# A two-layer streaming encoder on one core: the second attention's matmuls on halves of TensorE's rows

## The chip, the core and the metric

The kernel runs on one core of one Trainium2 chip. The metric is device microseconds of one execution. Within the core, TensorE (PE) multiplies, its weight loads (PEld) run beside its matmuls; VectorE (DVE), ScalarE (ACT) and GpSimd (POOL) work on tiles of 128 rows (partitions); SyncE (SP) issues most DMAs. Each engine works off its own list of instructions in order and waits on semaphores of the others. TensorE writes PSUM, which has eight banks of 128 x 512 fp32 values.

## The reference, cut to what matters

Layer A is a banded softmax attention, layer B a "stick-breaking" attention; both with gates, projections, residuals, and a prompt of 2048 frames beside a sample of 64 new frames with 2048 cached ones. The change touches layer B's attention and the two projections that run beside it. There are 16 heads of 64 numbers.

```python
def sb_block(q, k, v, q_pos, k_pos):
    z = jnp.einsum('bqhd,bkhd->bhqk', q, k).astype(jnp.float32) * SCALE
    mask = (k_pos[None, :] < q_pos[:, None])[None, None]
    log_fail = jnp.where(mask, jax.nn.log_sigmoid(-z), 0.0)
    later = jnp.flip(jnp.cumsum(jnp.flip(log_fail, -1), axis=-1), -1) - log_fail
    w = jnp.where(mask, jnp.exp(jax.nn.log_sigmoid(z) + later), 0.0)
    return jnp.einsum('bhqk,bkhd->bqhd', w.astype(v.dtype), v)
```

The kernel never forms `w`. With f = sigmoid(-z), the running product s of f from the newest key backwards holds the chance that no later key was taken, and `w` is a difference of neighbouring s. So the output is a sum of s against differences of neighbouring rows of v (made earlier and stored as `v_b`), plus the last row of v (`ends`).

## The kernel before

fp32 values are cut into a high and a low part, both fp32r, and a product is three products of parts. Layer B runs after its projections, from about 2040 us of the span on. The prompt's 2048 queries are four groups g of 512, its keys four chunks c of 512; groups come in two parts, (1, 0) and (3, 2), and in each part the loop is over eight pairs of heads (`hp`), then groups, then the two heads h, then chunks from c = g down to 0. After a part's groups comes a sample item of that pair, whose 64 queries of both heads fill one tile.

One `item(hp, g, h, ..., c)` has four tiles t of 128 queries. For each tile:

- `scores` makes z (128 x 512) with two matmuls over all 128 rows of the array. Rows 0 to 63 hold the high parts of the keys and rows 64 to 127 the low parts; the second matmul has the query's parts exchanged, so the four products of parts come out of two passes.
- `pass_sticks` (L1339) takes f = sigmoid(-z) on ACT, and, off the diagonal, three steps one beat apart: `pairs` on POOL multiplies neighbours (`two`, 256 values), `scan` on DVE runs the product over `two` backwards into every second value of s, `between` on POOL copies the carry and fills the other values (`s<-f,s`). On the diagonal (c = g) there is one scan over up to 512 values instead, and POOL does nothing. `own`, a constant that the scan also reads, lies in a PSUM bank.
- `weigh` turns four 128 x 128 blocks of s into a PSUM bank `wt` (the turnings, L90 `wt<-ident,s`), `split` copies it out as `ph` on ACT and the rest as `pl` on DVE, and `products` adds v times each into `acc`, one bank per head. `gate_steps` closes a head's `acc` into `ot`; POOL adds `ends` and multiplies by the gate.

Around this stand the "beside" products: the late k, q and g projections (`late_job`, `ps_j`) and the output projection (`out_tile`, `ps_o`), which a `Beat` object mixes in at a rate of `RATE["b"]` steps for each tile. `Beat.beat` writes the instructions of one beat: steps of older tiles, turnings, scores of the new tile, products, beside steps. `LAG`, `HOLD` and `LEAD` set how many beats lie between them. A scheduler then sets each engine's final order from what stands in the code, so the order shown below is that of the built program. PSUM holds three `wt` banks (beside products use them too), `own`, two z and two `acc`. All calls go through the recorder of L90, so most rows of the profile have that line.

## Time and profile before

| | us |
|---|---|
| runs shown | 3278.98 and 3283.02, median 3281.0 |
| span of the profiled execution | 3278.2 |
| profiled execution's own time | not listed apart; its span is 2.8 below the median of the runs |
| layer B's attention, from its first scores to its last products | 2040 to 3185, 1145 |
| what follows it: last output products, norm, stores | 3185 to 3279, 94 |
| TensorE busy over the span | 3204.2 (98%) |
| mean granted TensorE clock | 0.994 |

A row of the grouped view reads: line, engine, operation, out<-in by the program's names, shape, count, then busy microseconds and the mean nanoseconds of one, then the engine's idle time just before and what ended it. A row of the timeline reads: start, length (of all that are merged in it), engine, line, operation, names, shape, count, and in brackets the idle time before it with what ended it. `TENSOR_TENSOR_SCAN` in the profile is `SCALAR_TENSOR_TENSOR` with three inputs in the order of the program.

### The profile page before, as it was taken

The numbers are of one execution on the slowest core, as the hardware profiler recorded it, in microseconds if no ns is written. First come the engines' busy times: TensorE is split into PE (matmuls) and PEld (weight loads), VectorE is DVE, ScalarE is ACT, GpSimd is POOL, SyncE is SP. The second block draws the span as 40 slices with busy tenths as digits, with TensorE's granted clock in tenths as the row PEclk, the third lists the DMA queues.
The fourth block names the chain that finished last, engine by engine and source line by source line (L and its number), as shares of the span: only waits on it lengthen the run. The fifth ranks groups of instructions, "written<-read, shape, count | busy, mean of one in ns | idle before, by whom it ended". The sixth has DMA issues, their size and how long they took to land.

```text
span 3278.2 us, 53687 instructions
## 1 busy us (share of the span) xinstructions
PE 3204.2 (98%) x17928; PEld 2791.0 (85%) x17928; DVE 1887.0 (58%) x3786; ACT 1711.4 (52%) x3719; POOL 1291.4 (39%) x1950
## 2 busy tenths in 40 slices
PE   8999999999998999999999999999999989999999
PEld 7889999988887898878889998788888878888877
DVE  4235431147778775231044333788878878888873
ACT  5234222258888776143134442566666656666662
POOL 3001110026665554020044200444477766877761
PEclk9999999999999999999999999999999999999999
DMA  6359993387899983553399999977735566455423
GB/s 202 121 185 368 349 331 118 117 237 220 240 260 267 252 237 130 164 174 128 113 357 352 348 357 328 251 217 217 213 121 148 162 203 174 124 143 141 138 72 119
DMA packets 464892, 688.41 MB, mean 210 GB/s; under 512 B 51446, under 2 KB 261398, under 8 KB 464615
## 3 DMA queue, kind: packets, MB, share of 16 engines
q1 hardware_dynamic: 405158, 633.85, 61.8%
q10 hardware_dynamic: 59456, 51.13, 4.8%
q8 instruction: 143, 2.34, 0.3%
q14 instruction: 135, 1.10, 0.1%
HBM read 408.78 MB, written 276.07 MB: 209 GB/s over the span
## 4 chain that ended last, share of the span: by engine, by line
PE 75%; issue 7%; DVE 6%; DMA 6%; ACT 2%; POOL 2%; SPq 1%; POOLq 0%; ACTq 0%; DVEq 0%
PE ps_t L90 23%; PE ps_v L90 11%; PE acc L90 10%; PE z L90 9%; PE wt L90 8%; PE ps_j L90 6%; PE ps_o L90 5%; DVE s L90 3%; DVE pl L90 2%; DMA vt<-v_b 1%; PE ps_tr L90 1%; ACT ph L90 1%; DMA kt<-k_b 1%; POOL s L90 1%; ACT s L90 1%
## 5 line engine op out<-in xcount | busy, mean ns | idle before, releaser
L90 DVE TENSOR_TENSOR pl<-wt,ph 128x512 fp32r<-128x512 f32 (+1 forms) x864 | 551.9, 654 | 122.4 <-ACT ph L90 118.7
L90 ACT ACTIVATE ph<-wt 128x512 fp32r<-128x512 f32 (+1 forms) x864 | 485.7, 578 | 205.4 <-PE wt L90 178.2
L90 PE MATMUL ps_t<-x_own,wh 128*128 128x362 f32 (+1 forms) x2304 | 567.5, 327 | 0.0
L90 PE MATMUL wt<-ident,s 128*128 128x128 f32 x3472 | 551.5, 274 | 13.4 <-DVE pl L90 6.8
L90 PEld LDWEIGHTS wt<-ident,s 128*128 128x128 f32 x3472 | 418.6, 141 | 88.3 <-DVE pl L90 12.9
L90 ACT ACTIVATE f<-z 128x512 f32<-128x512 f32 (+4 forms) x680 | 355.1, 535 | 196.1 <-PE z L90 139.7
L90 PEld LDWEIGHTS ps_t<-x_own,wh 128*128 128x128 f32 x2304 | 405.0, 188 | 1.8
L90 POOL TENSOR_TENSOR s<-f,s 128x256 f32<-128x256 f32 x416 | 361.3, 870 | 104.2 <-DVE s L90 95.9
L90 PE MATMUL acc<-ph,vt 128*128 128x512 f32 (+3 forms) x1088 | 376.2, 381 | 14.1 <-DMA vt<-v_b 7.5
L90 PE MATMUL z<-kt,q 128*128 128x512 f32 (+3 forms) x1280 | 375.4, 381 | 12.9 <-DMA q<-q_b 5.8
L90 PE MATMUL ps_t<-x_own,wl 128*128 128x362 f32 (+1 forms) x1152 | 376.7, 327 | 0.0
L90 PE MATMUL acc<-pl,vt 128*128 128x512 f32 (+3 forms) x1088 | 364.6, 368 | 7.2 <-DVE pl L90 6.8
L90 POOL TENSOR_SCALAR s<-s,rc 128x640 f32<-128x640 f32 (+5 forms) x264 | 199.2, 760 | 387.3 <-DMA keys<-k_a 193.3
L90 PE MATMUL ps_o<-big,oh 128*128 128x512 f32 x1088 | 336.2, 392 | 0.2 <-ACT oh L90 0.2
L90 POOL TENSOR_TENSOR two<-f 128x256 f32<-128x256 f32 x416 | 259.5, 626 | 166.3 <-ACT f L90 150.0
L90 DVE TENSOR_TENSOR_SCAN s<-two,s,own 128x256 f32<-128x256 f32 x408 | 299.7, 738 | 33.6 <-POOL two L90 32.3
L90 PEld LDWEIGHTS z<-kt,q 128*128 128x128 f32 x1280 | 221.9, 192 | 43.5 <-ACT f L90 11.8
L90 PE MATMUL ps_j<-big,lwh 128*128 128x512 f32 x768 | 246.9, 397 | 1.1 <-DVE pl L90 0.6
L90 PE MATMUL ps_t<-big,wh 128*128 128x512 f32 x768 | 238.9, 391 | 0.0
L90 PEld LDWEIGHTS ps_o<-big,oh 128*128 128x128 f32 x1088 | 202.2, 188 | 41.3 <-ACT oh L90 0.4
L90 PEld LDWEIGHTS acc<-ph,vt 128*128 128x128 f32 x1088 | 198.7, 192 | 37.1 <-ACT ot L90 8.4
L90 DVE CUSTOM_DVE_ANT_0 s<-z,bias 128x640 f32<-128x640 f32 (+4 forms) x256 | 184.7, 733 | 77.2 <-PE wt L90 51.1
(148 smaller groups left out, 5528.9 us busy)
## 6 DMA issues: line engine op xcount, KB each, us to landing
vt<-v_b SPq DMA_DIRECT2D x80, 512.0 KB, 4.9
v_b<-vs SPq DMA_DIRECT2D x64, 512.0 KB, 5.7
q<-q_a SPq DMA_DIRECT2D x128, 256.0 KB, 5.9
q<-q_b SPq DMA_DIRECT2D x128, 256.0 KB, 4.6
vt<-v_a SPq DMA_DIRECT2D x48, 512.0 KB, 7.1
kt<-k_b SPq DMA_DIRECT2D x96, 256.0 KB, 5.6
keys<-k_a SPq DMA_DIRECT2D x80, 256.0 KB, 7.1
v_a<-vs ACTq DMA_DIRECT2D x32, 512.0 KB, 2.7
```

What stands on the lines that cost most here:

```text
L90: ins = op(*args, **kwargs)
```

## The change

In layer B, TensorE's array is used as two halves of 64 rows, `ROWS`. A matmul on rows 0 to 63 and one on rows 64 to 127 are written side by side by a small planner, `Array`, that keeps a clock for each half and takes the next piece of work of the half that is behind.

- Scores: the pair's two heads lie on the two halves. Each head has three matmuls over 64 rows (high-high, high-low, low-high), into the two banks of one z. One sigmoid covers both heads (128 x 1024), and s holds both heads.
- Turnings: a block is 64 queries by 128 columns, which a stride of 8 picks as 64 keys of each head; 16 half turnings take the place of 8 whole ones.
- Value products: rows 0 to 63 hold 64 keys of head 0 and rows 64 to 127 those of head 1, each into its own `acc` bank. v is loaded anew in that order (`spread`), and for the diagonal once more in other strides (`edges`, tile `vd`). On the diagonal a tile's products are 128 columns wide.
- Beside products: each half of the rows sums its share of K into one of two output banks, then the halves change places (`half_sums`, two phases); between the phases `meet` makes DVE read both banks.
- `pairs`, `scan` and `between` handle both heads: one POOL instruction over 2 x 255 values, a COPY of two, two scans, one POOL instruction over 512. s is written in place of f. A tile takes two beats (`gap=2`) instead of two tiles of one beat.
- z is one tile of two banks, `acc` has one buffer for each head, `own` moves from PSUM to SBUF; PSUM now holds three `wt`, z (2), `acc` (2) and `side`.
- Tables: `RATE` 0.3 to 0.6 (a step is half as large), `LAG` 5 to 3, `LEAD` 14 to 28, `HOLD` 2 to 1.

```diff
-RATE = dict(a=0.4, b=0.3)
-LAG = dict(a=3, b=5)
+RATE = dict(a=0.4, b=0.6)
+LAG = dict(a=3, b=3)
...
+ROWS = (slice(0, DH), slice(DH, P))
+TURN = 140
...
+    class Array:
+        def put(self, r, cost, what):
+            self.work[r].append((cost, what))
+        def product(self, r, out, w, x, **flags):
+            rows = ROWS[r]
...
+            self.put(r, n, lambda: mm(out, w[rows], x[rows], **flags))
+        def flip(self, r, out, in_):
+            rows = ROWS[r]
+            self.put(r, TURN, lambda: pe.transpose(out, in_[rows], ident[rows, rows]))
+        def run(self):
+            a, b = self.work
+            while a or b:
+                r = 0 if a and (not b or self.clock[0] <= self.clock[1]) else 1
+                cost, what = self.work[r].pop(0)
+                self.clock[r] += cost
+                what()
...
+    def pair_scores(z, q, kt, t, w):
+        for i, (x, y) in enumerate(((0, 0), (0, 1), (1, 0))):
+            for h in range(2):
+                array.product(h, z[:, h, :w], q[:, x, t * P : t * P + P], kt[:, y, :w], start=(i == 0), stop=(i == 2))
...
+    def half_sums(outs, phase, k, terms):
+        for r in range(2):
+            i = r ^ phase
+            these = terms(k, i * CH)
+            for j, (w, x) in enumerate(these):
+                array.product(r, outs[i][: w.shape[1]], w, x, ...)
+    def meet(outs):
+        for out in outs:
+            dve.tensor_copy(met, out[0:1, 0:1])
...
+    class PairBeat(Beat):
+        def beat(self, first=None):
+            for tile in list(self.tiles):
+                tile.pop(0)()
...
+            for block in self.blocks:
+                if block["turned"] < 2 and self.clock >= block["due"] + block["turned"]:
+                    block["turn"](block["turned"])
+                    after.append(partial(block["evict"], block["turned"]))
...
+            if first:
+                steps = first()
+                after.append(steps.pop(0))
+                self.tiles.append(steps)
...
+            array.run()
+            for x in after:
+                x()
...
+            for first in firsts:
+                self.beat(first)
+                for _ in range(gap - 1):
+                    self.beat()
...
-        own = psum.tile([P, CH], F32, name="own")
-        dve.tensor_copy(own, own_s)
-        KV, SB = 5, 12
-        banks.update(ph=4)
+        KV, SB = 4, 9
+        banks.update(ph=2)
...
             def pairs():
-                gps.tensor_tensor(two, by2[:, :, 0], by2[:, :, 1], ALU.mult)
+                gps.tensor_tensor(two[:, :, : CH // 2 - 1], f[:, :, 1 : CH - 1 : 2], f[:, :, 2:CH:2], ALU.mult)
+                gps.tensor_copy(two[:, :, CH // 2 - 1 :], f[:, :, CH - 1 :])
...
+            def scan_pairs(h):
                 dve.tensor_tensor_scan(
-                    to[:, CH - 2 :: -2], two[:, ::-1], own[:, : CH // 2], carry, ALU.mult, ALU.bypass
+                    f[:, h, ::-2], two[:, h, ::-1], own[:, : CH // 2], carry_in(h), ALU.mult, ALU.bypass
                 )
...
             def between():
-                gps.tensor_copy(to[:, CH : CH + 1], carry)
-                gps.tensor_tensor(to[:, 1:CH:2], by2[:, :, 1], to[:, 2 : CH + 1 : 2], ALU.mult)
+                gps.tensor_tensor(f[:, :, ::2], f[:, :, ::2], f[:, :, 1::2], ALU.mult)
...
+            return [take, pairs, lambda: [scan_pairs(h) for h in range(n)], between]
...
-                z = psum.tile([P, CH], F32, name="z", tag="z", bufs=2)
+                z, w = two_banks(), (t + 1) * P if c == g else CH
+                pair_scores(z, q, kv[0], t, w)
```

How the built program's order moves is shown at two places in the second part of the attention, groups (3, 2), off the diagonal. First POOL before: `two` is `pairs`, a COPY is the carry, `s<-f,s` is `between`; the number behind a name tells buffers apart.

```order
L90 TENSOR_TENSOR two_33538<-f_33536 128x256
L90 TENSOR_TENSOR s_33547<-f_33503,s_33547 128x256
L90 COPY s_33618<-s_33488 128x1
L90 TENSOR_TENSOR two_33561<-f_33559 128x256
L90 TENSOR_TENSOR s_33583<-f_33536,s_33583 128x256
L90 TENSOR_TENSOR ot_33253<-ot_33253,ends_21384 128x512
L90 TENSOR_TENSOR two_33595<-f_33593 128x256
L90 COPY s_33649<-s_33520 128x1
L90 TENSOR_TENSOR s_33618<-f_33559,s_33618 128x256
```

The `between` of one tile (f 33536) stands behind the `pairs` of the next tile (f 33559). Now POOL of the change; `s<-s` is `between`, in place.

```order
L93 TENSOR_TENSOR s_36693<-s_36693 128x512
L93 TENSOR_TENSOR two_36750<-s_36749 128x2x255
L93 COPY two_36750<-s_36749 128x2
L93 TENSOR_TENSOR s_36749<-s_36749 128x512
L93 TENSOR_TENSOR two_36811<-s_36810 128x2x255
L93 COPY two_36811<-s_36810 128x2
L93 TENSOR_TENSOR s_36810<-s_36810 128x512
```

Here a tile's `pairs` (s 36749) is followed by the same tile's `between`, and only then by the next tile's `pairs` (s 36810). The DVE side of the same tiles, of the change, with both heads' scans in one row:

```order
L93 SCALAR_TENSOR_TENSOR s_36749<-two_36750,s_36506,own_21367 128x256 x2
L93 TENSOR_TENSOR pl_36782<-wt_36789,ph_36781 128x8x64
L93 TENSOR_TENSOR pl_36831<-wt_36808,ph_36830 128x8x64
L93 SCALAR_TENSOR_TENSOR s_36810<-two_36811,s_36560,own_21367 128x256 x2
L93 TENSOR_TENSOR pl_36831<-wt_36838,ph_36830 128x8x64
```

Between the scans of two tiles stand two subtractions `pl`, as before for two heads' tiles. Second, TensorE, first before:

```order
L90 MATMUL wt_33491<-ident_69,s_33258 128x128
L90 MATMUL wt_33491<-ident_69,s_33280 128x128
L90 MATMUL wt_33491<-ident_69,s_33295 128x128
L90 MATMUL wt_33491<-ident_69,s_33332 128x128
L90 MATMUL acc_33275<-ph_33448,vt_32245 128x512
L90 MATMUL z_33500<-kt_33483,q_33382 128x512 x2
L90 MATMUL acc_33275<-pl_33449,vt_32245 128x512
```

And TensorE of the change; `acc0` and `acc1` are on different halves of the rows, and the eight `wt` of one bank are on one half:

```order
L93 MATMUL wt_36838<-ident_69,s_36454 128x64
L93 MATMUL wt_36838<-ident_69,s_36506 128x64
L93 MATMUL wt_36838<-ident_69,s_36560 128x64
L93 MATMUL wt_36838<-ident_69,s_36624 128x64
L93 MATMUL acc0_36562<-pl_36782,vt_35758 128x512
L93 MATMUL acc1_36563<-pl_36782,vt_35758 128x512
L93 MATMUL acc0_36562<-pl_36782,vt_35758 128x512
L93 MATMUL acc1_36563<-pl_36782,vt_35758 128x512
L93 MATMUL side_36280<-big0_32737,oh_35490 128x512
L93 MATMUL side_36279<-big0_32737,oh_35490 128x512
```

The products stand in pairs of opposite halves; the eight turnings ahead of them have no partner on the other half.

403 lines of the change are left out of this document (321 added, 82 removed).

## The prediction

> **What bounds the kernel now.** I read the stages by window first, then the grouped rows of layer B's attention, then single stretches of its timeline.
>
> ```profile
> core 0: us, PE busy (x) PEld busy (x) DVE busy (x) ACT busy (x) POOL busy (x), PEclk, DMA share, GB/s
> 2040.00:3185.00 1145.00, 1116.15 (x6378) 933.36 (x6378) 945.15 (x1527) 741.10 (x1506) 742.40 (x1350) 0.99 0.59 167
> 3185.00:3279.00 94.00, 85.91 (x388) 71.03 (x387) 34.82 (x64) 27.25 (x61) 16.59 (x21) 0.98 0.39 124
> ```
>
> In the 1145 us of layer B's attention TensorE is busy for 1116, DVE for 945, POOL for 742, at a granted clock of 0.99. A busy PE is not PE at its peak, so its work has to be counted.
>
> ```profile
> L90 PE MATMUL wt<-ident,s 128*128 128x128 f32 x2310 | 372.5, 274 | 2.2 <-DVE pl L90 1.1 <-POOL s L90 0.2
> L90 PE MATMUL z<-kt,q 128*128 128x512 f32 x896 | 289.9, 410 | 2.8 <-ACT f L90 2.2 <-DMA kt<-k_b 0.6
> L90 PE MATMUL acc<-ph,vt 128*128 128x512 f32 x448 | 201.6, 452 | 8.2 <-DMA vt<-v_b 7.5 <-ACT ph L90 0.6
> L90 PE MATMUL acc<-pl,vt 128*128 128x512 f32 x448 | 193.1, 431 | 6.5 <-DVE pl L90 6.1
> L90 PE MATMUL ps_j<-big,lwh 128*128 128x512 f32 x461 | 149.1, 397 | 0.4 <-DVE pp L90 0.3
> L90 PE MATMUL ps_o<-big,oh 128*128 128x512 f32 x288 | 92.1, 394 | 0.0
> L90 PE MATMUL ps_j<-big,lwl 128*128 128x512 f32 x231 | 91.6, 396 | 0.0
> L90 PE MATMUL ps_o<-big,ol 128*128 128x512 f32 x144 | 56.8, 395 | 0.0
> L90 PE MATMUL acc<-pp,vt 128*128 128x128 f32 x256 | 39.1, 276 | 1.1 <-DVE pp L90 1.1
> L90 PE MATMUL z<-kt,qs 128*128 128x512 f32 x96 | 28.7, 404 | 0.0
> ```
>
> The timeline gives what one matmul costs in a row of them, from start to start:
>
> ```profile
> 2863.98 0.40 PE L90 MATMUL ps_o<-big,ol 128*128 128x512 f32 x1
> 2864.21 0.62 PE L90 MATMUL ps_o<-big,oh 128*128 128x512 f32 x2
> 2864.67 0.39 PE L90 MATMUL ps_o<-big,ol 128*128 128x512 f32 x1
> ```
>
> Three beside products start from 2863.98 to 2864.67: 0.23 us for 512 columns.
>
> ```profile
> 2751.85 0.60 PE L90 MATMUL wt<-ident,s 128*128 128x128 f32 x4
> ...
> 3183.63 0.64 PE L90 MATMUL acc<-pp,vt 128*128 128x128 f32 x4
> ```
>
> Four whole turnings take 0.60 us, of which the last takes 0.27: 0.11 us each. Four 128-column products in a row: (0.64 - 0.276) / 3 = 0.12.
>
> The count for the stage: 512-column matmuls 896 + 448 + 448 + 461 + 288 + 231 + 144 + 96 = 3012, by 0.23 = 693 us; 2310 turnings by 0.11 = 254; 256 sample products by 0.12 = 31. The diagonal adds narrower ones: its scans, quoted below, come 64 times at each of 384, 256 and 128 columns, each with two matmuls for scores and two for products: 768 of 256 columns on average, at 512's 0.45 ns a column 88. Sum 1066 of 1145: TensorE is the bound, and 79 us are loss. DVE and POOL work beside it with slack.
>
> **The change, part by part.** All of it lies in the 1145 us, and a little in the 94 behind them.
>
> *TensorE.* If the two halves of the array work at once, a pair of half matmuls costs what one whole one does. Scores go from 4 passes for two heads to 3: 224 of the 896 go, and a quarter of the narrower ones (44 us): 62 us saved. Products off the diagonal and beside products keep their passes: nothing. On the diagonal 128-column products replace wider ones: 32 x 40 pairs by 0.06 (the columns' share) to 0.12 (the row above) = 77 to 154, where the old ones cost 44 + 128 x 0.23 = 73: 4 to 81 us more. A half turning is in the trace, where 64 sample rows are turned:
>
> ```profile
> 104.07 0.71 PE L90 MATMUL ps_tr<-ident,xt 64*128 64x64 f32 x8
> ...
> L90 PE MATMUL ps_tr<-ident,xt 64*128 64x64 f32 x16 | 1.4, 228 | 0.0
> ```
>
> (0.71 - 0.228) / 7 = 0.07 us. The program has 4624 of these in layer B, 324 us one after the other, half of that where the other half of the rows works meanwhile; 254 before. So TensorE's own work is 1066 - 62 + 42 - 11 = 1035 at the middle of these bounds, 920 to 1155. It would save about 30 us, if nothing else were late.
>
> *The chain through DVE and POOL.* The order shown has POOL do `pairs`, COPY, `between` of one tile before the next tile's `pairs`. `between` waits for that tile's scans, and the scans wait for `pairs` and COPY. Both engines go in order, so off the diagonal one tile of a pair costs scans + `between` + `pairs` + COPY, in series, whatever TensorE does. Before, the next tile's `pairs` stood ahead of `between`, so a scan had POOL work beside it.
>
> ```profile
> L90 POOL TENSOR_TENSOR s<-f,s 128x256 f32<-128x256 f32 x416 | 361.3, 870 | 104.2 <-DVE s L90 95.9 <-ACT f L90 3.9 <-ACT pp L90 1.8
> L90 DVE TENSOR_TENSOR_SCAN s<-two,s,own 128x256 f32<-128x256 f32 x408 | 299.7, 738 | 33.6 <-POOL two L90 32.3
> L90 POOL TENSOR_TENSOR two<-f 128x256 f32<-128x256 f32 x416 | 259.5, 626 | 166.3 <-ACT f L90 150.0 <-DVE s L90 13.6 <-DVE pl L90 2.3
> L90 POOL COPY s<-s 128x1 f32<-128x1 f32 x408 | 77.9, 193 | 53.2 <-DVE s L90 30.5 <-PE wt L90 22.6
> L90 POOL TENSOR_TENSOR ot<-ot,gt 128x512 f32<-128x512 f32 x31 | 40.7, 1313 | 0.1
> L90 POOL TENSOR_TENSOR ot<-ot,ends 128x512 f32<-128x512 f32 x31 | 32.9, 1060 | 5.9 <-DVE ot L90 5.9
> ```
>
> Two scans: 2 x 738 = 1.48 us. `between` on 512 values isn't in the trace: at least 1.06 (the cheapest 512-value product or sum of two inputs, `ends`), at most 2 x 870 = 1.74; I take 1.31, the row of `gt`, since it also is 512 values from two full inputs. `pairs` on 510: 1.06 (same lower row) to 1.25 (2 x 626); I take 1.06, which 626 also gives if a fixed part like COPY's 0.19 is paid once. COPY 0.19. Each hand-over:
>
> ```profile
> 2802.27 0.74 DVE L90 TENSOR_TENSOR_SCAN s<-two,s,own 128x256 f32<-128x256 f32 x1
> 2803.16 0.85 POOL L90 TENSOR_TENSOR s<-f,s 128x256 f32<-128x256 f32 x1 [1.25 <-DVE s L90]
> ...
> 2724.57 0.62 POOL L90 TENSOR_TENSOR two<-f 128x256 f32<-128x256 f32 x1
> 2725.23 0.75 DVE L90 TENSOR_TENSOR_SCAN s<-two,s,own 128x256 f32<-128x256 f32 x1 [0.38 <-POOL two L90]
> ```
>
> The scan ends at 3.01 and POOL starts at 3.16; `two` ends at 2725.19 and the scan starts at 2725.23. That is 0.19 a tile, less the 0.06 or so by which one instruction starts ahead of the last one's end: 0.1. Sum 1.48 + 1.31 + 1.06 + 0.19 + 0.1 = 4.14 us; bounds 3.8 and 4.85. The count: 416 rows are 2 x 192 for the prompt and 32 for the sample, so 192 x 4.14 = 795 us (730 to 931).
>
> *The rest of the stage, on the same chain.* The gating of 32 group outputs stands in POOL's line between these steps: 1.06 + 1.31 = 2.37 each, some two thirds of them in off-diagonal stretches, 50 us (0 to 76). A sample chunk: 0.63 + 0.19 + 0.87 + 0.74 + 0.1 = 2.53, 32 of them and 8 of new keys at about 2: 97 (90 to 110). On the diagonal DVE sets the pace:
>
> ```profile
> L90 DVE TENSOR_TENSOR pl<-wt,ph 128x512 fp32r<-128x512 f32 x512 | 337.2, 676 | 81.1 <-ACT ph L90 79.2
> L90 DVE TENSOR_TENSOR_SCAN s<-f,own 128x512 f32<-128x512 f32 x64 | 77.3, 1207 | 20.1 <-ACT f L90 20.0
> L90 DVE TENSOR_TENSOR_SCAN s<-f,own 128x384 f32<-128x384 f32 x64 | 60.1, 939 | 5.1 <-ACT f L90 4.9
> L90 DVE TENSOR_TENSOR ot<-acc,otmp 64x512 f32<-64x512 f32 x64 | 43.7, 682 | 5.9 <-ACT otmp L90 5.0
> L90 DVE TENSOR_TENSOR_SCAN s<-f,own 128x256 f32<-128x256 f32 x64 | 43.0, 671 | 5.7 <-ACT f L90 5.7
> L90 DVE TENSOR_TENSOR pl<-wt,ph 128x256 fp32r<-128x256 f32 x64 | 26.1, 408 | 1.9 <-ACT ph L90 1.5
> L90 DVE TENSOR_TENSOR_SCAN s<-f,own 128x128 f32<-128x128 f32 x64 | 25.5, 398 | 6.2 <-ACT f L90 6.2
> ```
>
> For one group of a pair 2 x (1207 + 939 + 671 + 398) ns of scans, 2 x (676 + 676 + 408) of subtractions, 2 x 682 to close: 11.3 us, by 32 = 362 (330 if some subtractions find DVE's gaps in the chain, 400 if TensorE's short products are later). `meet` adds 66 DVE copies, behind whose place in DVE's line the second phase of a beside sum waits, and turnings behind that: 0 to 40, I take 15, as the chain leaves TensorE idle anyway. Sum 795 + 50 + 97 + 362 + 15 = 1319 against 1145: 174 us more. Lead and tail: a beside sum drains once for `meet`, half a microsecond by the hand-overs, in some seven of them, and evicts later: 5.
>
> *What is priced at nothing.* One sigmoid of 1024 for two of 512: ACT is busy 741 of 1145. DMA: q is no longer stored twice (17 MB less), v's diagonal copy is 25 MB more, in pieces of 512 B, at a DMA share of 0.59 that falls with a longer stage; without that cover each late v costs what it did before, 8 us in all. Single z: the next scores come a beat after the sigmoid.
>
> *`own` in SBUF.* DVE's scan then reads two SBUF tensors. Here is a DVE subtraction of two SBUF tensors against POOL, with two `between` merged in the first row:
>
> ```profile
> 2750.42 1.68 POOL L90 TENSOR_TENSOR s<-f,s 128x256 f32<-128x256 f32 x2
> 2751.29 1.37 DVE L90 TENSOR_TENSOR ol<-og,oh 128x512 fp32r<-128x512 f32 x1
> ```
>
> POOL ends at 2752.10 and the subtraction at 2752.66, after 1.37 us, where the row of `pl` has 0.68 for this size: it waited for POOL's end. So such a DVE instruction and a POOL instruction exclude each other. As the chain already sets them in series, this adds nothing to 4.14 but for the gates (0 to 30, in their bounds); it forbids that a scan slips beside `between`.
>
> [...]
>
> Before this, 3278.2 of span: 3278 + 174 + 5 = 3457, and 3 for what lies between span and median: **3460 us**.
>
> **The rivals.** 2% is 66 us, about what a measurement of this kernel can tell from no change.
>
> *Chain near its floor.* All POOL prices at their lower rows: 192 x 3.8 + 0 to 50 + 90 + 330 = 1150 to 1200: 3290 to 3340. For it speaks that long instructions spread fixed costs; against it `between` with strided in and out, 870 for 256, the dearest of the rows. Chance 0.15, all of it within 2%.
>
> *TensorE stays the bound and gets faster.* It needs the chain below TensorE's share of a tile: 7 pairs by 0.23, turnings 0.84, beside work of 1.2 steps of 3 pairs 0.83, so 3.3 us, and POOL's three steps in 1.7 instead of 2.6. Then the stage is 1035 + 79, at the lower bound 920 + 79: 3250 to 3130. For it speaks that TensorE is the bound today; against it, that two 512-value POOL instructions have 2.1 as their lower bound. Chance 0.07, of which 0.05 faster by over 2%.
>
> *The halves don't work at once.* Then each half matmul costs 0.23: 512-column pairs 3012 - 224 - 128 = 2660, as halves 5320 x 0.23 = 1224, turnings 324, diagonal scores 68, diagonal products 154 to 307, sample 65: 1835 to 1990, and the 94 behind doubles: about 4140. The trace says nothing for or against. Chance 0.06.
>
> *Matmuls overlap, weight loads don't.* Four 128-column products in a row pay 0.12 each, more than their columns; if each half load costs that, 5320 + 2560 + 544 + 576 = 9000 loads by 0.12 = 1080 and 324 of turnings: 1404, with today's 79 of loss up to 1483: 3540 to 3630. Chance 0.12.
>
> **The numbers.** Forecast 0.60, with 3340 to 3700 as its own bounds (up to 931 + 76 + 110 + 400 + 40 = 1557 for the stage). Faster by over 2%: 0.05. Within 2%: the floor and the rest of the second rival, 0.17. Slower by over 2%: 0.78. The range 3310 to 3700 leaves out the halves one by one (0.06), the faster rival (0.07) and part of the floor (0.06).
>
> **What would show it.** Right: POOL and DVE rows in the attention alternate, `s<-s` idle before released by the DVE scan and `two` hard behind; PE idle before turnings released by POOL `s`; a tile every 4 to 4.3 us; the chain of waits led by POOL and DVE in this stage; PE starts of `acc0` and `acc1` within a few hundredths. Wrong: `s<-s` 128x512 below 1 us, PE still over 95% busy with short spacing, or pairs of halves starting 0.23 apart.

## The result, and the profile after

The changed kernel takes 3711.8 us (median of 2 runs, 3710.0 to 3713.5) against 3281.0: the ratio is 1.131, with an interval of 1.128 to 1.135. It is 431 us slower. The forecast was 3460, 179 slower, with 3310 to 3700 as its range. The sign holds; the size is 2.4 times the forecast.

The stages of the changed kernel by window: the lead and everything ahead as one row, layer B's attention, the tail (the same columns as before the change).

```profile
core 0: us, PE busy (x) PEld busy (x) DVE busy (x) ACT busy (x) POOL busy (x), PEclk, DMA share, GB/s
0.00:2040.00 2040.00, 1999.98 (x11142) 1788.07 (x11142) 898.43 (x2191) 939.26 (x2149) 532.75 (x580) 1.00 0.74 235
2040.00:3612.00 1572.00, 1445.03 (x13822) 1326.61 (x13823) 1000.72 (x1629) 755.76 (x1242) 570.56 (x778) 0.86 0.44 126
3612.00:3711.70 99.70, 84.97 (x704) 69.82 (x702) 32.00 (x72) 25.00 (x56) 12.91 (x16) 0.94 0.35 114
```

Nearly all of it lies in the attention: 1572 us where it was 1145, of which some 10 are a later start (VectorE's first scan of the stage starts at 2051.4 us for 2041.6). The tail has 100 us for 94. The new number in these rows is the granted clock: 0.86 where it was 0.99. Four short windows show what this is.

```profile
2117.50:2120.00 2.50, 2.50 (x22) 2.47 (x22) 0.69 (x1) 0.60 (x1) 0.00 (x0) 0.50 0.00 0
2120.00:2122.50 2.50, 2.50 (x22) 2.50 (x21) 0.69 (x1) 1.17 (x2) 0.00 (x0) 0.50 0.24 67
2142.50:2145.00 2.50, 2.50 (x40) 2.50 (x39) 1.98 (x3) 1.30 (x2) 0.90 (x3) 1.00 0.58 96
2145.00:2147.50 2.50, 2.50 (x41) 2.49 (x39) 0.77 (x2) 0.92 (x2) 1.70 (x3) 1.00 0.77 209
```

TensorE is busy from end to end in all four, but at clock 0.50 it starts 22 matmuls in 2.5 us and at 1.00 it starts 40. The page's row of clock tenths was all nines before; now most of the last 18 of its 40 slices, the attention and the tail, are 8s and 7s:

```profile
PEclk9999999999999999999999888879988899898789
```

The clock records of these traces hold only 1.00 and 0.50, so the time at half clock is 2 x (1 - granted clock) x span. With the whole run's clock of 0.940 that is 445 us (nearly all in the attention); with 0.994 before it was 39.

Off the diagonal the chain of the prediction is there. These are its rows by shape, and one tile in the timelines of GpSimd and VectorE:

```profile
L93 DVE TENSOR_TENSOR_SCAN s<-two,s,own 128x256 f32<-128x256 f32 x408 | 287.2, 740 | 307.5 <-POOL two L93 280.7 <-ACT ph L93 25.3
L93 POOL TENSOR_TENSOR two<-s 128x510 f32<-128x510 f32 x192 | 202.8, 1056 | 213.6 <-ACT s L93 212.4
L93 POOL TENSOR_TENSOR s<-s 128x512 f32<-128x512 f32 x192 | 200.6, 1045 | 324.5 <-DVE s L93 274.3 <-DVE total L93 19.2 <-DVE met L93 11.2
L93 POOL COPY two<-s 128x2 f32<-128x2 f32 x192 | 37.9, 197 | 0.0
```

```profile
2705.85 1.04 POOL L93 TENSOR_TENSOR s<-s 128x512 f32<-128x512 f32 x1 [1.60 <-DVE s L93]
2706.84 1.04 POOL L93 TENSOR_TENSOR two<-s 128x510 f32<-128x510 f32 x1
2707.82 0.19 POOL L93 COPY two<-s 128x2 f32<-128x2 f32 x1
2708.05 1.40 DVE L93 TENSOR_TENSOR_SCAN s<-two,s,own 128x256 f32<-128x256 f32 x2 [1.19 <-ACT ph L93]
2709.61 1.04 POOL L93 TENSOR_TENSOR s<-s 128x512 f32<-128x512 f32 x1 [1.60 <-DVE s L93]
```

From one `between` to the next are 3.76 us (2705.85 to 2709.61). GpSimd's wait for the scans is 1.60, and VectorE's scans start as COPY ends. The forecast was 4.14, with 3.8 as the lower bound: `between` takes 1.045 where I took 1.31, and `pairs` 1.056, as taken. But 3.76 is about the shortest such step, not the usual one. Of the 168 steps from one `between` to the next that are under 12 us (the longer ones have a diagonal or a sample item in them), 85 take 3.85 or less; their mean is 4.61. Where TensorE is at full clock for at least half of a step the median is 3.77, elsewhere 4.89.

The halves of the array do work at once. Here a score product on one half and a beside product on the other, in TensorE's timeline:

```profile
2705.15 0.39 PE L93 MATMUL side<-big,lwh 64*128 64x512 f32 x1
2705.19 0.39 PE L93 MATMUL z<-kt,q 64*128 64x512 f32 x1
2705.38 0.39 PE L93 MATMUL side<-big,lwh 64*128 64x512 f32 x1
2705.42 0.39 PE L93 MATMUL acc<-ph,vt 64*128 64x512 f32 x1
```

Two half products start within 0.04 us of each other, and the next two 0.23 later.

### The profile page after: what moved, and what is told of

Same layout as the page of the kernel before. It is cut to its first block, busy times and chain, and to the rows that moved or that the text cites. A ratio compares the mean times of both kernels' runs of the same rounds, so it can differ in the third digit from the quotient of the medians.

```text
span 3711.7 us, 67526 instructions
## 1 busy us (share of the span) xinstructions
PE 3530.0 (95%) x25664; PEld 3184.5 (86%) x25664; DVE 1931.2 (52%) x3891; ACT 1720.0 (46%) x3447; POOL 1116.2 (30%) x1374
## 4 chain that ended last, share of the span: by engine, by line
PE 68%; DVE 9%; issue 8%; POOL 7%; ACT 4%; DMA 4%; SPq 1%; POOLq 0%; ACTq 0%; DVEq 0%
PE ps_t L93 21%; PE acc L93 11%; PE ps_v L93 10%; PE wt L93 8%; PE z L93 7%; PE side L93 6%; DVE s L93 5%; POOL two L93 3%; ACT s L93 2%; POOL s L93 2%; PE ps_o L93 2%; PE ps_j L93 2%; DVE pl L93 1%; DVE ot L93 1%; POOL ot L93 1%
## 5 line engine op out<-in xcount | busy, mean ns | idle before, releaser
L93 PE MATMUL wt<-ident,s 64*128 64x64 f32 (+1 forms) x5784 | 791.0, 276 | 61.0 <-DVE pl L93 32.7
L93 PEld LDWEIGHTS wt<-ident,s 64*128 64x128 f32 (+1 forms) x5784 | 716.6, 187 | 123.7 <-DVE pl L93 48.2
L93 PE MATMUL z<-kt,q 64*128 64x512 f32 (+3 forms) x1920 | 443.4, 435 | 3.1 <-ACT s L93 3.1
L93 ACT ACTIVATE s<-z 128x1024 f32<-128x1024 f32 (+5 forms) x400 | 328.0, 820 | 175.9 <-PE z L93 161.2
L93 PE MATMUL acc<-pl,vt 64*128 64x128 f32 (+3 forms) x1728 | 380.0, 375 | 10.7 <-DVE pl L93 10.5
L93 PE MATMUL acc<-ph,vt 64*128 64x128 f32 (+3 forms) x1728 | 364.8, 363 | 6.7 <-ACT ot L93 5.7
L93 PEld LDWEIGHTS z<-kt,q 64*128 64x128 f32 x1920 | 316.9, 225 | 8.5 <-ACT s L93 4.1
L93 PE MATMUL side<-big,lwh 64*128 64x512 f32 x960 | 286.0, 461 | 11.2 <-DVE met L93 4.7
L93 PEld LDWEIGHTS acc<-pl,vt 64*128 64x128 f32 (+1 forms) x1728 | 254.1, 209 | 21.6 <-DVE pl L93 16.8
L93 PEld LDWEIGHTS acc<-ph,vt 64*128 64x128 f32 (+1 forms) x1728 | 243.6, 203 | 21.8 <-ACT ot L93 8.4
```

What stands on the lines that cost most here:

```text
L93: ins = op(*args, **kwargs)
```

## The experiments

Thirteen kernels. Each edit is against the changed kernel, and `...` marks lines left out. Of each run's spans, "diagonal" and "off the diagonal" are the attention cut at VectorE's scans: from the first scan of one kind to the first of the other. In the changed kernel the diagonal has 580 us of it and the rest, with the sample's chunks, 955; the same cut gives 408 and 721 in the kernel before, so both parts lost, 172 and 234 us.

**Newer tile first** (e1).

```
-            for tile in list(self.tiles):
+            for tile in reversed(list(self.tiles)):
```

> One word: the steps of the newer tile are taken first, so that on GpSimd `pairs` of tile t+1 stands ahead of `between` of tile t. Now a tile off the diagonal takes 3.77 us (two scans 1.40, `between` 1.04, `pairs` 1.04, COPY 0.18, hand-overs). Theory A, the chain is only a matter of order: scans of t+1 run beside `between` of t, GpSimd needs 2.27 and VectorE 2.66 a tile, TensorE (3.3 a tile by the prediction's sum) is the bound again, its idle windows go and with them the half clock: mean clock over 0.98, time 3200 to 3350. Theory B, scans with two SBUF inputs and GpSimd instructions exclude each other: 1.40 + 2.27 = 3.67 stay in series whatever the order, a tile takes 3.7 us, time 3650 to 3712 and mean clock about 0.94. Theory C, TensorE has more to do in halves than the prediction's 1035 us (its busy time weighted by the clock is 1250): the stage stays near 1250, time 3390 to 3480.

Measured: 3719.7 us. It tells apart nothing: GpSimd's order is not the code's order but the scheduler's, and in the trace GpSimd, VectorE and ScalarE have their instructions in the same order as in the changed kernel. The run is a repetition of it, 0.2% off, which also shows how far two such measurements lie apart.

**GpSimd's steps left out** (e2).

```
-                gps.tensor_tensor(two[:, :, : CH // 2 - 1], f[:, :, 1 : CH - 1 : 2], f[:, :, 2:CH:2], ALU.mult)
-                gps.tensor_copy(two[:, :, CH // 2 - 1 :], f[:, :, CH - 1 :])
...
-                    f[:, h, ::-2], two[:, h, ::-1], own[:, : CH // 2], carry_in(h), ALU.mult, ALU.bypass
+                    f[:, h, ::-2], f[:, h, ::-2], own[:, : CH // 2], carry_in(h), ALU.mult, ALU.bypass
...
-                gps.tensor_tensor(f[:, :, ::2], f[:, :, ::2], f[:, :, 1::2], ALU.mult)
```

> Leaves out GpSimd's `pairs`, COPY and `between` of the off-diagonal tiles; the scan runs in place over every second value (two scans of 256, as now), so the sticks passed are wrong there. No GpSimd work is left in a tile, so neither order nor exclusion can hold TensorE back: what is left is TensorE's own sum. If that is the prediction's 1035 us with 79 of losses: stage 1110, time 3240 to 3270, clock over 0.98. If TensorE has more to do in halves (1250): 3390 to 3480. If the diagonal and the short first groups are held by VectorE (362 us) whatever happens elsewhere: 3300 to 3380.

Measured: 3517.9 us (one execution), above every value expected. The attention by window:

```profile
2040.00:3416.00 1376.00, 1312.15 (x13842) 1234.98 (x13839) 1018.81 (x1632) 754.28 (x1243) 106.05 (x108) 0.92 0.50 145
```

With no GpSimd work in any tile the attention takes 1376 us, 231 more than before the change, at a clock of 0.92. So GpSimd's part of the chain, taken out alone and with what its waits did to the clock, is worth 196 us; the larger part of the loss stays without it.

**Filler in TensorE's waits** (e4).

```
+    def fill(r, wt):
...
+        wide = identr.unsqueeze(1).to_broadcast([P, 4, P])
+        for _ in range(2):
+            array.put(r, CH, lambda: mm(wt, identr, wide, start=True, stop=True))
...
             wt = bank("wt")
+            fill(r, wt)
```

> Adds work: ahead of each group of turnings of a pair's half two whole-array products of 128x512 (identity on identity) into the same bank, which the turnings then overwrite; 576 x 2 x 0.23 = 265 us of TensorE time at full clock, standing just where it waits for the sticks. Theory A or B with the clock (440 us of the stage at half clock, each time after a window of 3.4 us in which TensorE was below some 0.88 busy): the filler runs in the waits and keeps the windows full, the mean clock rises from 0.94 to over 0.97, and time falls, by 50 to 150 us, to 3560 to 3660, although work was added. If the half clock costs nothing because the chain sets the pace anyway: unchanged or some 20 to 60 us slower, 3712 to 3770. Theory C (TensorE's own work is the bound): 265 us slower, 3900 to 3980.

Measured: 4260.3 us, 548 slower, above every value expected, and the clock at 0.946 hardly higher. TensorE's timeline, at full clock:

```profile
2951.11 0.39 PE L93 MATMUL side<-big,lwl 64*128 64x512 f32 x1
2951.43 0.73 PE L93 MATMUL wt<-identr 128*128 128x512 f32 x2
2952.09 0.50 PE L93 MATMUL acc<-pl,vt 64*128 64x512 f32 x1
```

From the start of the last half product before them to the next half one are 0.98 us. The half product's own columns are 0.23 of it, so the two whole ones cost 0.75, where two cost 0.46 in a row of their kind. The filler was no free work, so the run doesn't tell what the clock costs. It did show that half products next to whole ones cost extra: here 0.75 - 0.46 = 0.29 us for the two changes around a pair of whole ones.

**An order edge on GpSimd** (e5).

```
-            for tile in list(self.tiles):
+            for tile in reversed(list(self.tiles)):
...
-                gps.tensor_copy(two[:, :, CH // 2 - 1 :], f[:, :, CH - 1 :])
+                latest[0] = gps.tensor_copy(two[:, :, CH // 2 - 1 :], f[:, :, CH - 1 :])
...
-                gps.tensor_tensor(f[:, :, ::2], f[:, :, ::2], f[:, :, 1::2], ALU.mult)
+                with tc.issue_after(latest[0].ins):
+                    gps.tensor_tensor(f[:, :, ::2], f[:, :, ::2], f[:, :, 1::2], ALU.mult)
```

> The same wish as the run that took the newer tile first, which left every engine's order as it was; now an edge makes `between` of tile t issue behind `pairs` and COPY of tile t+1 on GpSimd. `own` stays in SBUF. If a scan (two SBUF inputs) and a GpSimd instruction exclude each other, 1.40 + 2.27 stay in series: a tile takes 3.7 us as now, time 3690 to 3715, clock 0.94. If they don't, the scans of t+1 run beside `between` of t, the chain falls to 2.7 a tile, and time goes towards that of the run without GpSimd's steps (3518): 3500 to 3560.

Measured: 3778.5 us, 67 slower than without the edge and outside both ranges expected. Now `between` of one tile and the scans of the next start together, in GpSimd's and VectorE's timeline:

```profile
2723.11 1.04 POOL L93 TENSOR_TENSOR two<-s 128x510 f32<-128x510 f32 x1 [2.22 <-ACT s L93]
2724.10 0.19 POOL L93 COPY two<-s 128x2 f32<-128x2 f32 x1
2724.24 1.04 POOL L93 TENSOR_TENSOR s<-s 128x512 f32<-128x512 f32 x1
2724.32 2.15 DVE L93 TENSOR_TENSOR_SCAN s<-two,s,own 128x256 f32<-128x256 f32 x2 [1.06 <-POOL two L93]
```

Two scans take 2.15 us, where they took 1.40 without GpSimd beside them. So a scan does wait for `between`, as the exclusion in the prediction says. Each `between` now also ends a tile later; that this is the 67 us is not shown.

**Turnings on whole rows** (e6).

```
-            n = 0
-            for ws, _, _ in blocks():
-                for w in ws:
-                    array.flip(r, wt[:, n : n + DH], w)
-                    n += DH
...
+            ws = [w for part, _, _ in blocks() for w in part]
+            m = len(ws) // 2
+            for i, w in enumerate(ws[r * m : r * m + m]):
+                array.put(r, TURN, partial(flip, wt[:, i * P : i * P + P], w))
...
```

> Undoes one part: the prompt's turnings work on all 128 rows again (four 128x128 into a bank for eight 64x64), all else as after. From windows at full clock a half turning costs 0.074 us and a whole one 0.116 before, so 4096 halves by 0.074 (303) become 2048 by 0.116 (238): 65 us less TensorE work. The half clock comes where fewer than some 2730 columns, each counted by its share of the rows, start in a window of 3.41 us; a whole turning counts 128, two half ones 64. So if that count is what the clock goes by, time at half clock falls well below 440 us (to 150 to 300), and time is 65 plus half of what goes: 3480 to 3600. If the chain through GpSimd sets the pace whatever TensorE does: 3690 to 3715.

Measured: 3948.7 us, 237 slower, at a clock of 0.929. Both expectations fall. The 2730 of the first is an estimate that fits the changed kernel's own trace: of its 951 windows of 3.41 us at full clock 55 are followed by half clock, and this limit misplaces 9; m1 below contradicts its count of the turnings. Whole turnings are no dearer by themselves (m1 below: 0.109 for one, 0.11 to 0.13 for two half ones), but each group of them stands between half products. By m1 a change between whole and half costs 0.2 us; 576 groups with two changes each would be 230 us, an estimate that nearly covers the loss.

**Beside products on whole rows** (e7).

```
-RATE = dict(a=0.4, b=0.6)
+RATE = dict(a=0.4, b=0.3)
...
-LEAD = dict(a=8, b=28)
+LEAD = dict(a=8, b=14)
...
-        if L == "b":
+        if False:
             products = [partial(halves, i, k0) for i in range(2) for k0 in range(NK)]
...
```

> Undoes one part: beside products on all rows, one bank after the other, rate and lead of before, so no `meet` and no `side` bank; scores, turnings and products of the attention stay in halves. The columns are the same. If `meet` and the drain between phases cost what the prediction has (15 + 5) and nothing else changes: 3690 to 3700. [...]

Measured: 3726.6 us, 15 slower (0.4%, not far above the 0.2% of e1), clock 0.944, and above the 3690 to 3700 expected. So beside products in halves, `meet` and its waits aren't where the time went: what they cost is no more than what whole products between half ones cost.

**Scores alone in halves** (e8): e7's edit, `own` in PSUM, the order edge of e5, and turnings and value products as they were before.

```
-                        array.product(
-                            h,
-                            acc()[h][:, c0 : c0 + m * P],
...
+                    mm(
+                        acc()[h][:, c0 : c0 + m * P], vs[h], st[s][:, h, at : at + m],
...
-            packs = [(1,), (2, 0), (3,)] if c == g else [(0,), (1,), (2,), (3,)]
+            packs = [(0,), (1, 3), (2,)] if c == g else [(0,), (1,), (2,), (3,)]
```

> Only the scores of a pair work in halves (3 passes for two heads instead of 4); turnings, value products, the diagonal's layout and beside products are on all rows as before, `own` is in PSUM as before, one sigmoid and 512-value GpSimd steps for a pair as after, and `between` is issued behind the next tile's `pairs`. TensorE's sum is 1066 - 62 = 1004 us, all of it counted in full by the clock, so no half clock beyond before's 31 us. If TensorE is the bound: 3210 to 3270, faster than both kernels. If scans and GpSimd stay in series (3.7 a tile) even with `own` in PSUM: stage 724 + 50 + 97 + 362 = 1233, time 3370 to 3400. If the single z bank pair holds the scores back: 3290 to 3340.

Measured: 3465.7 us, above every value expected and 188 slower than the kernel before measured with it, at a clock of 0.984. With nearly all work on whole rows most of the half clock goes (some 111 us are left of 445), and 246 us of the loss with it; but the 62 us that the scores save don't show. What else holds this kernel isn't taken apart: in its waits the scores wait 96 us for the sigmoid to free the one pair of z banks.

**Single costs** (m1). Its edit is a kernel of its own, rows of independent instructions:

```
    ROW = (slice(0, 64), slice(64, P))
    QUARTER = slice(0, 32)
...
    for _ in range(150):
        mm("d_quarter", QUARTER, CH)
...
    for _ in range(300):
        for r in ROW:
            mm("h_narrow", r, P)
...
    for _ in range(60):
        mm("i_mix", ALL, CH)
        mm("i_mix", ROW[0], CH)
        mm("i_mix", ROW[1], CH)
```

> Leaves the encoder out: the outputs are zeros, and single costs are measured by themselves. TensorE runs rows of independent matmuls, 64 whole 512-column products ahead of a row to bring the clock up: whole products (a), products on one half of the rows alone (b), on both halves in turn (c), on a quarter of the rows (d), whole turnings (e), half turnings on one half (f) and on both in turn (g), 128-column half products on both in turn (h), one whole and two half products in turn (i), a half product against two turnings on the other half (j). Rule 1, the clock goes by columns counted by their share of the rows, with a limit of some 2730 in 3.41 us: (b) counts 3845 and stays at 1.00, (d) counts 1920 and falls to 0.50 although TensorE never waits, (e) 3970 stays, (f) at 0.065 us counts 1680 and falls, (g) counts 1480 at 0.074 a turning, 3360 at 0.0325: falls in the first case. Rule 2, it goes by TensorE's waiting: all stay at 1.00. Costs: a pair in (c) 0.23 if halves work at once, 0.46 if not; (g) 0.074 a turning as in the kernel or half of (f); (i) 0.64 a group if each change between whole and half costs 0.09, else 0.46; (j) 0.23 a group if turnings and products of the other half work at once. VectorE and GpSimd: scans of 256 with two SBUF inputs 0.70 alone and up to 1.5 beside `between`, which stays at 1.04; with the second input in PSUM 0.70 in both.

TensorE's timeline, one row of it for each stretch (the letter in a name is the one in the text):

```profile
22.40 34.16 PE L93 MATMUL a_whole<-x,w 128*128 128x512 f32 x150
56.49 33.86 PE L93 MATMUL b_onehalf<-x,w 64*128 64x512 f32 x148
90.65 34.19 PE L93 MATMUL c_halves<-x,w 64*128 64x512 f32 x298
139.52 61.08 PE L93 MATMUL d_quarter<-x,w 32*128 32x512 f32 x150
217.17 32.91 PE L93 MATMUL e_wturn<-ident,raw 128*128 128x128 f32 x300
264.56 31.87 PE L93 MATMUL f_hturn<-ident,raw 64*128 64x64 f32 x500
311.11 27.96 PE L93 MATMUL g_hturns<-ident,raw 64*128 64x64 f32 x500
353.74 38.43 PE L93 MATMUL h_narrow<-x,w 64*128 64x128 f32 x600
406.72 51.93 PE L93 MATMUL i_mix<-x,w 128*128 128x512 f32 x180
```

Whole products take 0.227 us each, products on one half 0.227, and pairs of half products 34.19 / 149 = 0.229: the halves work at once without loss. A whole turning takes (32.91 - 0.27 for the last one's own length) / 299 = 0.109; a half turning 0.064 alone and 0.056 when the halves alternate, so two half turnings, which do the work of a whole one, cost 0.11 to 0.13. Half products of 128 columns take 38.43 / 600 = 0.064 each on alternating halves, 0.128 a pair, where a whole one takes 0.06 to 0.12 from start to start in the trace before the change: here the halves gain nothing. And a group of one whole and two half products takes 51.93 / 60 = 0.87 where 0.46 is the work: each of the two changes in it costs 0.2. What it is spent on is not shown. In (j) a half product with two half turnings on the other half takes 0.278 a group, for 0.227 and 2 x 0.064 = 0.128 alone: turnings and products of opposite halves overlap in part. The windows of (d) and of (h):

```profile
146.00:200.00 54.00, 54.00 (x128) 40.94 (x127) 0.00 (x0) 0.00 (x0) 0.50 0.70 264
353.80:392.00 38.20, 38.20 (x601) 38.20 (x600) 0.00 (x0) 0.00 (x0) 1.00 0.01 2
```

On a quarter of the rows the clock is at 0.50 although TensorE is busy for 54.00 of 54.00 us: rule 2 falls. Rule 1 falls as I had counted it, since (f) and (g) stay at 1.00. It fits all of these stretches if a turning's columns are counted twice, which is my estimate: (f) then has 64 in 0.064 us, 3430 in a window of 3.41 us. With that count, seven of these traces (the changed kernel, e2, e5 to e9) were cut into windows of this length: of 6744 at full clock 301 were followed by half clock, and a fitted limit of 3010 columns, each by its share of the rows, tells them from the others with 30 misplaced. With columns counted in full whatever their rows, the best limit misplaces 149; with TensorE's busy share in place of columns, 163. In six traces that had no part in the fit (before, e1, e10 to e13) the same 3010 misplaces 26 of 5774, and the best limit on the busy share 135.

VectorE and GpSimd in the same run, scans beside `between`: first with both of the scan's inputs in SBUF, then with the second one in PSUM:

```profile
48.90 26.29 DVE L93 TENSOR_TENSOR_SCAN sc<-two,own 128x256 f32<-128x256 f32 x20
49.65 38.67 POOL L93 TENSOR_TENSOR h<-g 128x512 f32<-128x512 f32 x30
88.54 14.38 DVE L93 TENSOR_TENSOR_SCAN sc<-two,ownp 128x256 f32<-128x256 f32 x20
88.83 33.53 POOL L93 TENSOR_TENSOR h<-g 128x512 f32<-128x512 f32 x30
```

20 scans with both inputs in SBUF take 26.29 us beside `between` (1.35 each, after the first two, which take 0.69 each) and 14.38 with the second one in PSUM (0.69 each). Thirty `between` take 38.67 and 33.53. So the two hold each other up as the prediction has it, though not for their whole length, and this goes when `own` is in PSUM. With both inputs in SBUF a scan and a `between`, which take 0.69 and 1.04 alone, start every 1.38 us in pairs, longer than either alone and less than the 1.73 of both.

**Beside products to the diagonal, and away from it** (e9, e10).

```
         def item(hp, g, q, gt, kv, acc, carry, c):
             tiles = {}
+            beat.rate = 1.2 if c == g else 0.25     # e9
+            beat.rate = 0.3 if c == g else 0.75     # e10
```

> The rate of beside products is 1.2 steps a beat on diagonal blocks and 0.25 elsewhere, for 0.6 throughout (423 steps in all for 432): the dense 512-column products go where half turnings and 128-column halves are, and where the clock is at half most. TensorE's work is the same. If the half clock comes from too few counted columns and costs what the trace says (440 us at half, 220 us lost): half-clock time falls to 150 to 300 us, time 3580 to 3660. If the chain through GpSimd or the diagonal's own chain sets the pace: 3700 to 3740, as the off-diagonal stretches lose their filler and wait.

> The opposite of the run with dense diagonals: 0.3 steps of beside products a beat on diagonal blocks, 0.75 elsewhere, for 0.6 throughout; TensorE's work is the same. With 1.2 on the diagonal its stretches grew from 580 to 669 us and the others shrank from 955 to 917 only. If the diagonal is bound by TensorE and the off-diagonal tiles by the chain of 3.77 us, which leaves TensorE some room: the diagonal falls to 480 to 540, the rest stays within 955 to 990, time 3630 to 3690. If the diagonal is paced by VectorE, as the prediction has it: unchanged there, the rest longer, 3712 to 3740.

Measured: e9 3765.3 us at a clock of 0.932, diagonal 669, off it 917; e10 3683.1 at 0.945, diagonal 559, off it 949. Dense products didn't bring the clock up in e9; they lengthened the diagonal, which has no room for them. Away from it they gain 29 us (21 on the diagonal, 6 off it). Of the expectation for e10 the time came true, the diagonal's 480 to 540 did not. So the diagonal is held by TensorE, at least in part, and off it TensorE has some room.

**One part of the diagonal's value products left out** (e11).

```
         def products(s):
+            if s >= parts:                          # 1 on the diagonal, else 2
+                return
```

> Leaves out the second (low) part of the value products on the diagonal, so that the outputs there lack precision: 1280 half products of 128 columns fewer, at 0.064 us each (measured alone) 82 us of TensorE time at full clock, 164 at half; every other engine does what it did. If the diagonal is paced by VectorE (11.3 us a group in the prediction): its stretches stay at 580 us and time at 3700 to 3715. If by TensorE: 400 to 500 us, time 3550 to 3630, below 3630 where the half clock goes with it.

Measured: 3669.9 us, 42 faster, diagonal 553. It lies between the two: 82 us of TensorE work less give 27 us on the diagonal and 20 behind it. VectorE doesn't pace the diagonal alone, and TensorE doesn't either.

**More columns in the same instructions** (e12): each value product of the diagonal streams its columns twice.

```
-                            acc()[h][:, c0 : c0 + m * P],
+                            acc()[h][:, c0 : c0 + n * m * P],        # n = 2 on the diagonal, else 1
...
-                            st[s][:, u : u + m].rearrange("p m r q -> p (m r q)"),
+                            st[s][:, u : u + m].rearrange("p m r q -> p (m r q)").unsqueeze(1).to_broadcast([P, n, m * P]),
```

> Adds columns, in the same order of instructions: each value product of the diagonal streams its 128 columns twice, into 256 columns of the bank, so that a neighbouring query tile gets these sums too. 128-column half products measured alone cost 0.064 us each, and the 256-column ones of the scores here 0.06, so TensorE's work at full clock is the same within some 20 us, while the columns counted for these 1536 products double. If the half clock follows the count and costs time: half-clock time in the short first groups falls by 100 to 200 us and time by 40 to 100, to 3610 to 3670, though more columns are worked. If the clock costs nothing, because chains through the other engines set the pace: 3705 to 3740.

Measured: 3674.1 us, 38 faster, with nothing removed and 2560 products twice as wide (the expectation counts 1536; the trace has 2560 more half products of 256 columns and as many fewer of 128). The attention:

```profile
2040.00:3572.00 1532.00, 1383.41 (x13839) 1264.29 (x13836) 1000.76 (x1632) 756.45 (x1243) 570.78 (x780) 0.93 0.45 131
```

The clock is 0.93 for 0.86, and over the run 0.965 for 0.940: 257 us at half clock for 445. So in this run more columns in the same instructions went with more of the full clock and with less time: 38 us for 188 us of half clock, 0.2 each. It isn't 0.5, what a granted clock of 0.50 takes where TensorE is busy throughout (in the short windows above it started 22 matmuls for 40); that part of the half clock lies where TensorE would have waited is the likely reason, not a shown one. Executions of one and the same kernel say something similar. In e13 one of the four had 239 us of half clock and a span of 3624.4 us, the others 292 to 299 and 3644.9 to 3650.3. Over the nine of these kernels with four executions each, a microsecond more of half clock goes with 0.37 us more of time (in e5 alone with none). Which of the two brings the other this can't tell.

**The chain broken** (e13): e7's edit, then e5's edge and

```
-        own = wpool.tile([P, CH], F32, name="own")
...
+        own = psum.tile([P, CH], F32, name="own")
+        dve.tensor_copy(own, own_s)
```

> To be read against the run with whole beside products (3727), which frees a bank: `own` back in PSUM and `between` issued behind the next tile's `pairs`. Measured alone, a scan with its second input in PSUM takes 0.69 beside GpSimd, where with both in SBUF each pair of a scan and a `between` takes 1.39. So the serial 3.77 us a tile become 2.3 on GpSimd and 2.7 on VectorE. If that chain is what makes TensorE wait off the diagonal: the off-diagonal stretches fall from 955 to 800 to 870 us and time to 3580 to 3660. If TensorE's own work with the half clock sets the pace there as well: 3700 to 3730.

Measured: 3649.0 us against e7's 3726.6, clock 0.960 for 0.944, off the diagonal 894 for 955. Two scans beside `between`, in the two engines' timeline:

```profile
2714.26 1.04 POOL L93 TENSOR_TENSOR s<-s 128x512 f32<-128x512 f32 x1
2714.34 1.39 DVE L93 TENSOR_TENSOR_SCAN s<-two,s,own 128x256 f32<-128x256 f32 x2
```

They take 1.39 us again, for 2.15 in e5. Order and `own` together gain 78 us, with what the waits did to the clock; the time is in the range expected, the 894 is above its 800 to 870. The order alone (e5) made it slower, and `own` in PSUM alone was not run. With the chain broken the steps from `between` to `between` go down to 2.1 us and less in a tenth of the cases, but their mean is 3.97, so something else holds most of them. Of the kernels whose attention works in halves throughout and leaves nothing out it is the fastest, and it is 371 us behind the kernel before measured with it.

No version here beats the kernel before: in halves TensorE's own work is larger than before (next section), and mixing whole and half rows costs 0.2 us a change.

## Why the prediction was right in sign and wrong in size

**TensorE's sum** was the first step that failed. The prediction has 1035 us for the changed kernel and 1066 before. The 1035 holds only if the halves work at once, which no row of the trace before shows; in m1 they do (0.229 us for a pair of half products, 0.227 for a whole one). With the costs measured alone, and the counts of both traces, before is 3012 x 0.227 + 2310 x 0.109 + 103 for the narrower ones by their columns = 1039, so the method was good. After it is 5452 half products of 512 columns x 0.1145 = 624, 4624 half turnings x 0.064 = 296, 3296 of 128 columns x 0.064 = 211, 384 between these widths 27: 1158.

So TensorE's work rose by 119 where the prediction has 31 less; with 0.12 for each of the sample's whole products, as in the prediction, before is 1054 and the rise 104. Two terms make up 101 of the 123 us by which the prediction's 1035 fell short; the other 27 of the 150 between -31 and 119 are that 1066 was more than this count gives for the kernel before. Half turnings were priced at "324 us one after the other, half of that where the other half of the rows works meanwhile", and I took the middle, 243; in m1 they gain little from each other (0.056 for 0.064), and it is 296. Narrow value products on the diagonal were taken at 116 us for 1280 pairs, and are 164: the upper bound, 0.12 a pair, was the right row, and slightly too low.

The rival that weight loads don't overlap fits the products of 128 columns, where the weight loads are busy for all of window (h), and not those of 512, so its 0.12 a load was too high everywhere. No run sets loads apart from products, so for the narrow ones the cause stays open.

**The clock** is the term that the prediction doesn't have at all. I read 0.99 and 0.98 in the windows and kept them. But the change makes TensorE wait (busy for 1445 of 1572 us in the attention, for 1116 of 1145 before) and puts its work on half the rows, and time at half clock goes from 39 to 445 us. The stretches at 0.50 in the changed kernel that end before its last instruction are 3.41 us long or a multiple of it, up to 34.1. In the 51 windows of that length ahead of a drop in its attention TensorE is busy for 0.09 to 0.87 of the time, 0.68 at the median. The prediction has no such term, since in the trace of before the half clock came to 39 us. It prices `meet` at little "as the chain leaves TensorE idle anyway", but each of the 51 drops came after a window in which TensorE waited, and what such a wait costs the work behind it is not shown apart. What TensorE does at 0.50 can be seen in its timeline:

```profile
2116.40 0.41 PE L93 MATMUL acc<-ph,vd 64*128 64x128 f32 x1
2116.41 0.37 PE L93 MATMUL wt<-ident,s 64*128 64x64 f32 x1
2116.61 0.41 PE L93 MATMUL acc<-pl,vd 64*128 64x128 f32 x1
2116.62 0.36 PE L93 MATMUL wt<-ident,s 64*128 64x64 f32 x1
2116.82 0.41 PE L93 MATMUL acc<-pl,vd 64*128 64x128 f32 x1
```

Each 0.21 us hold one product of 128 columns on half the rows and one half turning: 64 columns each by the count above, 128 in 0.21 us, 2080 in 3.41 us, below the fitted 3010. Of the 125 windows of 3.41 us at half clock in the attention, 74 were followed by another one, with 2528 columns by that count at the median, and 51 by full clock, with 3584; TensorE's median busy share was 1.00 in both. So by this estimate it takes no wait to stay at half clock: such work of the diagonal counts too little, until denser work comes. Before, whole turnings and wider products stood there.

**The chain** was right in its mechanism and its order, 3.77 us for 4.14, and 192 tiles at that pace are 724 us for 795. What was wrong is "whatever TensorE does": only half of the steps keep that pace (85 of 168 take 3.85 or less), and their mean is 4.61. TensorE's sum is 120 us larger, and the clock is at half for over a quarter of the time; at half clock the step's median is 4.89. Without GpSimd's steps 196 us come back (e2), without the serial order and the exclusion 78 (e13). The exclusion itself, read from two rows, was right in the main (m1, e5), though in m1 a scan and a `between` do overlap, by 0.35 of 1.73 us.

**The diagonal** was the second step that failed: "On the diagonal DVE sets the pace", 11.3 us a group, 362 in all, with 400 as the upper bound. The stretches are 580, with eight chunks of new keys in them. In the second part of the stage (from 2558 us) they are 14.7 us each, with VectorE busy 0.83: nearest to the prediction. In the first part, where short groups bring narrow products and few dense ones, they are 21.1 us each, with VectorE busy 0.58 and TensorE 0.95, at half clock for 0.35 of the time: there TensorE is the busy engine, not VectorE.

**The account.** 1572 us in the attention, 1145 before: TensorE's own work 1158 for 1039 (+119); half of the half-clock time, by the windows' clock 0.14 x 1572 = 220 for 11 (+209); the rest, waits and unpaired halves, 194 for 95 (+99). The middle term is an upper bound for what the clock costs, since part of it hides waits: by e12 a microsecond at half clock cost 0.2, by which 400 more would be 80, and by the executions of one kernel 0.37, by which they would be 150. How the 310 us beside TensorE's own work split between clock and waits isn't settled; e2, e12 and e13 show that each is there, and in e2 and e13 the clock rose as waits went. Lead and tail were right: 5 forecast, 6 measured.

**The rivals.** The halves work at once, so 4140 was wrong. That weight loads are serial gave 3540 to 3630 and came nearest, with a mechanism that the narrow products alone can bear out; that its number came near is luck, since it has neither the chain nor the clock. TensorE faster, 3130 to 3250, and the floor, 3290 to 3340, went the wrong way. The range missed by 12 us at the upper end: its cases held the clock fixed.

## What to carry to other kernels

Cost a packing of half the rows by its narrowest pieces, not by its 512-column ones: there the halves paired up without loss (0.229 us a pair for 0.227), but 128-column products (0.128 a pair for 0.06 to 0.12) and turnings (0.11 to 0.13 for 0.109) gained nothing, and the granted clock was 0.86 in the attention where it had been 0.99. Where a change makes TensorE wait or its work thinner, put the granted clock into the sum as a term of its own; here an estimate from the columns and rows that start in each window of 3.41 us told the drops from the rest (30 of 6744 misplaced). And before moving an operand between PSUM and SBUF, look at which two engines then read SBUF with two inputs in the same stretch: here a scan and a `between` then took 1.38 us a pair.

## What the runs showed of the hardware

- On 32 of 128 rows, busy for 54.00 of 54.00 us, TensorE was granted 0.50 (m1, d); on 64 rows of 128, also without a gap, 1.00 (m1, b, c, f, g, h). An estimate, fitted to seven traces: half clock came after windows of 3.41 us with fewer than some 3010 columns started, each by its share of the rows and a turning's twice. In six others it misplaces 26 of 5774 windows.
- With the columns of 2560 narrow products doubled the kernel was 38 us faster, at a clock of 0.965 for 0.940 (e12).
- A change between products on whole and on half rows cost 0.2 us (m1, i), and undoing the halves in one place only did not help (e6 237 us slower, e7 15).
- A scan with two SBUF inputs and a GpSimd product took 1.38 us a pair, for 0.69 and 1.04 alone; with one of the scan's inputs in PSUM they kept 0.69 and 1.04 beside each other (m1).
